# Retention heads' small steps over 14 slots, q's decay in the norm's epsilon, block sums moved into the convolution, two plain groups first

## The chip, the cores and the metric

The program runs on one core of one Trainium2 chip. The time is that of the core in microseconds (us), from the device's own record. The kernel before takes 3146.97 us, the median of three runs. The engines are TensorE (PE in the profile: matmuls; PEld: its weight loads), VectorE (DVE), ScalarE (ACT), GpSimd (POOL) and SyncE (SP), which issues most DMAs from one queue, in order.

## The reference

A decoder trunk of two layers over 2048 positions of width 1024, in float32. Each layer is h + norm(mixer(norm(h))).

The first layer's mixer multiplies the normed input by one weight matrix and splits the columns into 8 retention heads (q and k of 64 columns, v and a gate of 128) and 1024 short-convolution channels (cb, cc, cx and a gate). A head rotates q and k by position, works in chunks of 128 positions and carries a state of 64 x 128:

```
scores = einsum('bnihd,bnjhd->bnhij', qc, kc) * intra      # decay inside a chunk
inner  = einsum('bnhij,bnjhe->bnihe', scores, vc)
cross  = einsum('bnihd,nbhde,hi->bnihe', qc, prev, xi)     # xi[i] = gamma^(i+1)
r = rms_norm(inner + cross, gn)                            # per position and head, eps 1e-6
```

r times silu(gate), beside cb * conv3(cc * cx) * silu(gate), goes through an output matrix. The second layer is latent attention with 8 heads; the change does not touch it.

## The kernel before, in words

**Products.** The input projection is made in groups, Q = 0 to 63. Groups 0 to 31 are the heads: four pairs of heads (768 columns: two times 384) by eight blocks of 256 rows. Groups 32 to 63 are the convolution: 2 x 8 x 2 groups with 512 columns a half. A group multiplies a 2 x 2 block matrix by a 2 x 2 block matrix and needs seven block products instead of eight (`PROD`: P1, P4, P5, P3, P6, P2, P7), because sums of blocks are multiplied: S1 to S4 of the left side, T1 to T4 of the right. P4 and P3 of a group are made during the next group. Each float32 operand is split into a high and a low part (`split`: ScalarE copies the high part, VectorE subtracts), and a product is 4 x 3 = 12 matmuls (`mm12`, lines 87 to 89).

**Slots.** The order is written out by hand. A slot is one product plus all that is listed for its number: `T0(Q)` is the number of group Q's first slot, seven slots to a group. `step` issues the product and then `slot`: first the small matmuls listed in `pe_ev`, then `prep` (the low part of the left operand for 4 slots ahead, line 308; the high part for 5 ahead, line 300; its load 8 ahead, lines 283 to 290), then the list `events`, then `retention_engine`, then the second halves (`en`) of the small steps. Every engine runs its own part of this in order and waits where it needs another's result. The left operands pass through a ring of nine tiles (`us`). For groups 0 to 7 they are taken from SBUF (`RA`, `SS`), later from DRAM (`a_d`, `s_d`), and for the convolution from `wc_d` (a copy of the weights) and `ws_d` (their sums).

**Weights and sums.** `change` loads and splits the right operands of the next head pair or convolution half around its first group. `job` makes block sums on GpSimd: a load into a tile (w9 or j8 in turn), four additions of 512 columns (lines 373 and 374), a store. Kind "r" makes the T of head pairs, "u" the T of the convolution's right side (the normed input, read from `ub_d`), "w" the S of the convolution's weights. From group 8 a job starts every 4 slots. `cps` copies weights from DRAM to DRAM, one every 4 slots from slot 8.

**The heads' small steps.** Each group gives two units (one per head). Of a unit, `post` rotates q and k on VectorE (lines 512 to 518) and prepares v and the gate (519 to 522); `tr` transposes q and k (527, 528) and moves them out of PSUM: q times its decay xi on VectorE (542), k on ScalarE (543); `score` (551 to 564) makes scores and the chunk's addition to the state; `inner` (572, 573, 585 to 587) makes the outputs and the norm's sum of squares, with `eps` as a constant; `mixed` (593) scales; the transposes at 533 turn the result around, and `mix_tr` copies it out (600) and stores it from GpSimd's queue (601). In slots counted from the next group's first: post in 2 and 4, transposes in 4 and 7, scores in 5 and 8, inner in 7 and 11. So scores follow the transposes by one slot. `g1` puts transposes of one unit, output transposes and inner of others into one break of the products.

**The start.** Group 0 is made of eight plain products (`rows0`) while the input x is normed (`x_rstd`, `x_norm`), transposed (468) and copied out (672), 256 rows to a group; the T of the first head pair are made on GpSimd (760), stored to `wt_d` and loaded back. Groups 1 to 7 get their x tiles the same way some 14 slots ahead; `a_store` writes them to `a_d` and once more, by blocks, to `ub_d` (476).

## Time and profile before

| | |
|---|---|
| median of three runs | 3146.97 us |
| profiled execution | 3142.59 us |
| its span, first to last instruction | 3140.8 us |
| mean granted TensorE clock | 0.984 |
| heads, until the third product of group 32 | 797 us |
| convolution's last product | about 1414 us |

The profile shows one execution. A row of groups reads: line, engine, operation, output<-inputs, shape, xcount | busy us, mean ns of one | idle time before them and what ended it. A row of waits reads: who waited <- for whom: us in total, times, longest. A timeline row begins with its start and duration. A stretch's row gives, per engine, busy us and the number of instructions, then the granted clock (1.00 is full speed), the busy share of the 16 DMA engines and GB/s. SPq and ACTq are the issuing of DMAs on those engines.

### The profile page before, as it was taken

The page shows a single profiled execution, that of the slowest core. Times are in us where ns is not written, and L with a number is a line of the kernel's source. Part 1 is how long each engine was busy: PE and PEld are TensorE (multiplying, and loading weights), DVE is VectorE, ACT ScalarE, POOL GpSimd, SP SyncE. Part 2 cuts the span into 40 slices and gives each one's busy share as a digit, 9 for nine tenths or more (in the row PEclk, how much of TensorE's full clock was granted, in tenths as well). Part 3 has the DMA queues.
Part 4 walks back from the last instruction along what each step waited for, and adds up shares of the span by engine and source line. Part 5 has one row for each costly group of instructions (what it writes and reads, how often), then busy time and mean ns, then how long its engine had stood idle before and what let it go on. Part 6 is the DMA issues. An engine that isn't in the chain of part 4 may idle for free.

```text
span 3140.8 us, 46345 instructions
## 1 busy us (share of the span) xinstructions
PE 2999.4 (95%) x16413; PEld 2628.3 (84%) x16413; DVE 1862.5 (59%) x3687; ACT 1337.0 (43%) x3218; POOL 877.9 (28%) x1271
## 2 busy tenths in 40 slices
PE   4898988889999999998999999999999999999999
PEld 4787877789788888887888888998899999999887
DVE  5777888887655565545333311558666666666643
ACT  4544444445533353334222321343555555555521
POOL 4465666662100000000111110014333333333311
PEclk8999999999999999999999999999999999999999
DMA  6688898974433453336333542426321211212552
GB/s 240 231 274 277 291 326 298 343 258 148 154 110 111 144 171 111 109 94 212 127 121 108 162 145 72 123 82 212 114 66 60 66 52 63 63 51 68 169 162 87
DMA packets 279879, 477.05 MB, mean 152 GB/s; under 512 B 27840, under 2 KB 163664, under 8 KB 274896
## 3 DMA queue, kind: packets, MB, share of 16 engines
q1 hardware_dynamic: 254128, 390.43, 38.7%
q0 software_dynamic: 25200, 83.38, 7.3%
q8 instruction: 130, 2.13, 0.3%
q14 instruction: 101, 0.83, 0.1%
q10 hardware_dynamic: 320, 0.29, 0.0%
HBM read 327.20 MB, written 170.66 MB: 159 GB/s over the span
## 4 chain that ended last, share of the span: by engine, by line
PE 77%; DVE 7%; issue 7%; DMA 5%; POOL 3%; ACT 1%; SPq 1%; POOLq 0%; DVEq 0%; ACTq 0%
PE y L966 11%; PE bx L87 5%; PE fy L1738 5%; PE bx L89 5%; PE bx L88 5%; PE T L1543 4%; PE by L87 2%; PE by L88 2%; PE by L89 2%; PE o L1573 2%; PE o L1572 2%; PE o L1571 2%; PE S L1490 2%; PE S L1493 2%; PE S L1494 2%
## 5 line engine op out<-in xcount | busy, mean ns | idle before, releaser
L1511 POOL TENSOR_SCALAR P<-P,al 128x512 f32<-128x512 f32 (+2 forms) x320 | 218.7, 693 | 353.8 <-DVE al L1516 168.3
L308 DVE TENSOR_TENSOR us<-us 128x512 fp32r<-128x512 f32 x392 | 300.9, 777 | 8.0 <-ACT us L300 4.8
L1501 ACT ACTIVATE P<-S,nm 128x512 f32<-128x512 f32 (+2 forms) x320 | 200.8, 627 | 197.1 <-DVE nm L1498 173.4
L300 ACT CAST us<-us 128x512 fp32r<-128x512 f32 x392 | 233.2, 624 | 70.2 <-DMA us<-s_d 52.1
L1498 DVE TENSOR_REDUCE nm<-S 128x1 f32<-128x512 f32 (+2 forms) x320 | 194.3, 608 | 71.2 <-PE S L1494 43.3
L368 ACT COPY u<-bx 128x512 f32<-128x512 f32 (+1 forms) x126 | 67.1, 533 | 307.1 <-PE bx L89 306.9
L1547 DVE TENSOR_TENSOR TL<-T,TH 128x512 fp32r<-128x512 f32 x224 | 154.3, 689 | 63.4 <-ACT TH L1546 62.2
L1571 PE MATMUL o<-TH,vH 128*128 128x256 f32 x576 | 185.1, 321 | 0.0
L966 PE MATMUL y<-woH,mH 128*128 128x512 f32 x512 | 159.9, 394 | 8.9 <-ACT woH L82 8.9
L1543 PE MATMUL T<-ident,P 128*128 128x128 f32 x1088 | 166.2, 273 | 0.0
L1573 PE MATMUL o<-TH,vL 128*128 128x256 f32 x576 | 162.9, 283 | 0.0
L1572 PE MATMUL o<-TL,vH 128*128 128x256 f32 x576 | 162.1, 282 | 0.0
L966 PE MATMUL y<-woH,mL 128*128 128x512 f32 x512 | 158.5, 391 | 0.0
L966 PE MATMUL y<-woL,mH 128*128 128x512 f32 x512 | 157.6, 389 | 0.0
L83 DVE TENSOR_TENSOR mL<-mr,mH 128x512 fp32r<-128x512 f32 (+1 forms) x72 | 45.3, 631 | 170.0 <-ACT mH L82 170.0
L1546 ACT CAST TH<-T 128x512 fp32r<-128x512 f32 x224 | 131.0, 585 | 24.2 <-PE T L1543 18.6
L899 POOL DMA_DIRECT2D mix_d<-j x32 | 17.3, 540 | 441.2 <-DVE j L898 441.2
L1543 PEld LDWEIGHTS T<-ident,P 128*128 128x128 f32 x1088 | 125.1, 140 | 7.8
L966 PEld LDWEIGHTS y<-woH,mH 128*128 128x128 f32 x512 | 95.4, 189 | 28.2 <-ACT woH L82 9.3
L1490 PE MATMUL S<-kH,aqn 128*128 128x512 f32 (+2 forms) x320 | 118.4, 370 | 0.1
L82 ACT CAST mH<-mr 128x512 fp32r<-128x512 f32 (+1 forms) x72 | 40.9, 569 | 176.3 <-issue 93.6
L1493 PE MATMUL S<-K,aqr 128*128 128x512 f32 (+2 forms) x320 | 115.4, 361 | 0.0
(566 smaller groups left out, 9357.2 us busy)
## 6 DMA issues: line engine op xcount, KB each, us to landing
us<-ws_d SPq DMA_DIRECT2D x128, 256.0 KB, 2.9
us<-s_d SPq DMA_DIRECT2D x96, 256.0 KB, 6.0
us<-wc_d SPq DMA_DIRECT2D x96, 256.0 KB, 2.6
us<-a_d SPq DMA_DIRECT2D x72, 256.0 KB, 6.0
wc_d<-in_even_w_conv SPq DMA_DIRECT2D x32, 512.0 KB, 5.8
qn_d<-qn POOLq DMA_DIRECT2D x32, 512.0 KB, 3.2
aqn<-qn_d SPq DMA_DIRECT2D x64, 256.0 KB, 3.1
mr<-mix_d SPq DMA_DIRECT2D x56, 256.0 KB, 2.7
```

The source lines that it names most:

```text
L87: PE.matmul(o, ah, bh, start=first, stop=False, **kw)
L88: PE.matmul(o, ah, bl, start=False, stop=False, **kw)
L89: PE.matmul(o, al, bh, start=False, stop=last, **kw)
L300: A.copy(ring[n_][:, 0], f32(ring[n_][:, 1]))
L308: V.tensor_tensor(out=t_[:, 1], in0=src, in1=f32(t_[:, 0]), op=ALU.subtract)
L966: PE.matmul(ys[t][i], a, w[k][:, i * 512:(i + 1) * 512], start=first and pi == 0, stop=last and pi == 2)
L1501: later(D_EXP, lambda: A.activation(p_[:, 0:w], sp[:, 0:w], AF.Exp, bias=nm[:, j:j + 1], accum_out=sm[:, j:j + 1]))
L1511: G.tensor_scalar(t_[:, 0:ww], t_[:, 0:ww], al[:, jj:jj + 1] if n > 1 else al[:, 5:6], al[:, 5:6] if n > 1 else 1.0, op0=ALU.mult, op1=ALU ...
L1543: PE.transpose(tp[:, e, z, :], src, ident)
L1571: PE.matmul(hold[i], vH[h][:, kb, :], pth[:, c], start=first, stop=False)
L1572: PE.matmul(hold[i], vH[h][:, kb, :], ptl[:, c], start=False, stop=False)
L1573: PE.matmul(hold[i], vL[h][:, kb, :], pth[:, c], start=False, stop=last)
```

## The change

- The first two groups, not one, are plain products; the seven-product scheme begins with group 2. The sums S of groups 0 and 1 are made in place on GpSimd after their products' operands have been split (`s_op0`), and the T of the first head pair on VectorE (`t_op`). The norm's weights are loaded first, from ScalarE's queue, and the second x tile before the projection weights.
- The decay xi of q is no longer multiplied in. A row of the output is then larger by 1/xi, and the norm divides that out if its epsilon is scaled by 1/xi^2: a table `c_epsx` replaces the constant. q leaves PSUM by two ScalarE copies.
- A unit's steps are listed over 14 slots: transposes in 3 and 6, scores in 5 and 8, inner in 7 and 10, output transposes of two units together in 9, `mixed` in 8 and 13. Outputs are stored from ScalarE's queue, and the tile vh has two buffers instead of three. The transposes of x (468) use the PSUM bank that product P2 writes (`a`) instead of that of the q and k transposes.
- Jobs start every 7 slots instead of every 4; fourteen of them (ten "w", four "u") start after the heads, every 5 slots, in tiles of their own.
- `ub_d` is gone: what was read from it is read from `a_d` in pieces of 512 bytes. The copies of weights are made shortly before use, and half of the second row's copies is left out.

```diff
-    c["c_xi"] = ((g[:, None] ** (i + 1.0)) * DK ** -0.5).astype(np.float32)
+    c["c_epsx"] = (EPS * DK / g[:, None] ** (2.0 * (i + 1.0))).T.astype(np.float32).copy()
...
-        for Q in range(1, NQ_ + 1):
+        for Q in range(2, NQ_ + 1):
...
-        T0 = lambda Q: 7 * (Q - 1)
+        T0 = lambda Q: 7 * (Q - 2)
...
-                    SP.dma_start(flat(L), ub_d[tb, j, :, k0 * 512:(k0 + nk) * 512])
+                    for uu in range(2):
+                        for c in range(2):
+                            o = (2 * uu + c) * P
+                            SP.dma_start(L[:, :, o:o + P], a_d[2 * tb + uu, :, 2 * c + j, k0 * P:(k0 + nk) * P].rearrange("p (k c) -> p k c", k=nk))
...
             def a_store(Q):
                 SP.dma_start(a_d[Q].rearrange("p z c -> p (z c)"), RA[Q].rearrange("p z k c -> p (z k c)"))
-                for z in range(4):
-                    c, j = divmod(z, 2)
-                    o = (2 * (Q % 2) + c) * P
-                    SP.dma_start(ub_d[Q // 2, j].rearrange("p (k t) -> p k t", k=4)[:, :, o:o + P], RA[Q][:, z])
...
-                vh = bp.tile([P, 2, P], F32, tag="vh", bufs=3, name=f"vh_{s}")
+                vh = bp.tile([P, 2, P], F32, tag="vh", bufs=2, name=f"vh_{s}")
...
-                    V.tensor_tensor(out=qT[r, c, :], in0=pt[r, 0, :], in1=xi_[h % 2][r, :], op=ALU.mult)
+                    A.copy(qT[r, c, :], pt[r, 0, :])
                 A.copy(kT, pt[:, 1, :])
...
-                G.tensor_scalar(ss, ss, 1.0 / DV, EPS, op0=ALU.mult, op1=ALU.add)
+                G.tensor_scalar(ss, ss, 1.0 / DV, epsx[:, h:h + 1], op0=ALU.mult, op1=ALU.add)
...
+            def mix_tr(v, pt):
+                lo = 0 if v[0] is not None else 2
+                hi = 4 if v[1] is not None else 2
+                mxo = bp.tile([P, 4, P], F32, tag="mxo", bufs=1, name=f"mxo{v[0]}_{v[1]}")
+                A.copy(mxo[:, lo:hi], pt[:, lo:hi, :])
+                for i, s in enumerate(v):
+                    if s is not None:
+                        h, u = units[s]
+                        A.dma_start(mix_d[h * P:(h + 1) * P, u * 256:(u + 1) * 256], mxo[:, 2 * i:2 * i + 2].rearrange("p c t -> p (c t)"))
...
+            for p in range(RQ):
+                a_, b_ = 2 * p, 2 * p + 1
+                b = T0(p + 1)
+                if p >= 2:
+                    late(T0(p) + 5, lambda p=p: sum_a(p))
+                    late(b, lambda p=p: sum_y(p, 1, 1, "u3"))
+                    late(b + 1, lambda p=p: A.copy(pjt[0][:, 1, :], banks(p, "x")))
+                    late(b + 3, lambda p=p: sum_y(p, 1, 0, "u2"))
+                at(b + 2, lambda a_=a_: post(a_))
+                at(b + 4, lambda b_=b_: post(b_))
+                small(b + 3, *step_tr(a_))
+                small(b + 5, *step_score(a_))
+                small(b + 6, *step_tr(b_))
+                small(b + 7, *step_inner(a_))
+                late(b + 8, lambda a_=a_: mixed(a_))
+                small(b + 8, *step_score(b_))
+                small(b + 10, *step_inner(b_))
+                late(b + 13, lambda b_=b_: mixed(b_))
+                small(b + 9, *step_mix((a_, b_ - 2 if p else None)))
...
-            js += [("w", q_, 0) for q_ in range(8)] + [("u", 1, k) for k in range(4)] + [("w", q_, 0) for q_ in range(8, 16)]
+            js += [("w", q_, 0) for q_ in range(6)]
             for i, (kd, a_, b_) in enumerate(js):
-                job_at(T0(8) + 3 + 4 * i, job(kd, a_, b_, (w9, j8)[i % 2]))
+                job_at(T0(8) + 3 + 7 * i, job(kd, a_, b_, (w9, j8)[i % 2]))
...
-            cps = [(wh_d[h, j], w_heads[h, j]) for hp in range(1, 4) for h, j in ((2 * hp, 0), (2 * hp, 1), (2 * hp + 1, 1))]
-            cps += [(wc_d[o * 8 + ct], w_conv[o * 8 + ct]) for ct in range(8) for o in (2, 1, 3, 0)]
-            for i, (o, a_) in enumerate(cps):
-                at(8 + 4 * i, lambda o=o, a_=a_: SP.dma_start(o, a_))
+            for hp in range(1, 4):
+                for i, (h, j) in enumerate(((2 * hp, 0), (2 * hp, 1), (2 * hp + 1, 1))):
+                    at(T0(8 * hp) - 40 + 6 * i, lambda h=h, j=j: SP.dma_start(wh_d[h, j], w_heads[h, j]))
+            for q_ in range(16):
+                g_, ct, w = CQ[q_]
+                o0, o1 = (o * 8 + ct for o in COFF[w])
+                at(T0(RQ + q_) - 25, lambda o0=o0: SP.dma_start(wc_d[o0], w_conv[o0]))
+                at(T0(RQ + q_) - 22, lambda o1=o1: SP.dma_start(wc_d[o1, 1], w_conv[o1, 1]))
...
             x_load(0)
+            A.dma_start(gpre, pbc(pre_norm[0], D))
             SP.dma_start(ident, c_ident)
-            SP.dma_start(gpre, pbc(pre_norm[0], D))
+            x_load(1)
...
+            def t_op(n_):
+                o, a_, b_ = {"T1": ("B11", "B12", "B11"), "T3": ("B12", "B22", "B12"), "T2": ("B22", "B22", "B11"), "T4": ("B21", "B21", "B22")}[n_]
                 for half in range(2):
+                    c = slice(768 * half, 768 * half + 768)
+                    V.tensor_tensor(out=raw0[o][:, c], in0=raw0[a_][:, c], in1=raw0[b_][:, c], op=ALU.subtract)
+                SP.dma_start(wt_d[0, :, TIX[n_]].rearrange("p k c -> p (k c)"), raw0[o])
...
+            for Q in range(2):
+                C0 = {(c, h): psb.tile([P, 512], F32, tag="xy"[c], bufs=2, name=f"b0{Q}{c}{h}")[:, 0:384] for h in range(2) for c in range(2)}
+                for i, (c, j, h) in enumerate(rows0):
...
+                    mm12(C0[c, h], q0[Q, c, j], lambda k: (H[:, k, :], L[:, k, :]), j == 0, j == 1, False)
+                    early(Q, i)
+                    slot(8 * Q + i - 16)
...
+            jc = [cp.tile([P, 3072], F32, tag="u8", bufs=1, name="jc0"), cp.tile([P, 2048], F32, name="jc1")]
+            for i, (kd, a_, b_) in enumerate([("w", q_, 0) for q_ in range(6, 16)] + [("u", 1, k) for k in range(4)]):
+                job_at(LAST_SMALL + 1 + 5 * i, job(kd, a_, b_, jc[i % 2]))
```

More of the change, by code (lines that the diff above doesn't have):

```diff
@@ L110, in body @@
     wc_d = dram.tile([32, 2, P, 512], F32, name="wc_d")
-    ub_d = dram.tile([4, 2, P, 2048], F32, name="ub_d")
     ws_d = dram.tile([16, P, 4, 512], F32, name="ws_d")
@@ L392, in load @@
                     for z in range(4):
-                        SP.dma_start(t_[:, z], ub_d[2 * a + z % 2, z // 2, :, b * 512:(b + 1) * 512])
+                        j, tb = z // 2, 2 * a + z % 2
+                        for uu in range(2):
+                            src = a_d[2 * tb + uu].rearrange("p (c j) (k t) -> p c j k t", j=2, t=P)[:, :, j, b, :]
+                            SP.dma_start(t_[:, z, uu * 256:(uu + 1) * 256].rearrange("p (c t) -> p c t", c=2), src)
             def store():
@@ L418, in body @@
             qk_ = [bp.tile([P, 2, 2, 64], F32, name=f"qk{i}") for i in range(2)]
-            xi_ = [bp.tile([P, P], F32, name=f"xi{i}") for i in range(2)]
+            epsx = bp.tile([P, HR], F32, name="epsx")
             pjt = [bp.tile([P, 2, 384], F32, name=f"pj{i}") for i in range(2)]
@@ L442, in s_place @@
                 sj["t"] = w_new(7, F32, "sj")
-                SS.update({Q: QB(sj["t"]) for Q in range(1, 7)})
+                SS.update({Q: QB(sj["t"]) for Q in range(2, 7)})
             at(-5, s_place)
@@ L528, in tr_pe @@
                 PE.transpose(pt[:, 1, :], qk[:, 1].rearrange("p c d -> p (c d)"), ident)
-            def mix_pe(s, pt):
-                mc = st.pop(s)["mc"]
-                for c in range(2):
-                    PE.transpose(pt[:, 2 + c, :], mc[:, c, :], ident)
             def tr(s, pt):
@@ new lines, in step_mix, with pe @@
+            def step_mix(v):
+                def pe():
+                    pt = psb.tile([P, 4, P], F32, tag="tr", bufs=1, name=f"tm{v[0]}_{v[1]}")
+                    for i, s in enumerate(v):
+                        if s is not None:
+                            mc = st.pop(s)["mc"]
+                            for c in range(2):
+                                PE.transpose(pt[:, 2 * i + c, :], mc[:, c, :], ident)
+                    return pt
+                return pe, lambda pt: mix_tr(v, pt)
@@ L633, in unit, with step_score, step_inner @@
+            def step_score(s):
+                return lambda: score_pe(s), lambda _: score(s)
+            def step_inner(s):
+                return lambda: inner_pe(s), lambda _: inner(s)
             def unit(s):
                 return s if 0 <= s < NU else None
-            for Q in range(RQ):
-                a_, b_ = 2 * Q, 2 * Q + 1
-                base_t = T0(Q + 1)
-                tail_ = Q == RQ - 1
-                small(base_t + 4, g1(a_, unit(a_ - 1), unit(a_ - 2)))
-                if a_:
-                    at(base_t + 5, lambda a_=a_: mixed(a_ - 1))
-                at(base_t + (7 if tail_ else 8), lambda a_=a_: mixed(a_))
-                small(base_t + 5, (lambda a_=a_: score_pe(a_), lambda _, a_=a_: score(a_)))
-                small(base_t + (6 if tail_ else 7), g1(b_, a_, unit(b_ - 2)))
-                small(base_t + (7 if tail_ else 8), (lambda b_=b_: score_pe(b_), lambda _, b_=b_: score(b_)))
@@ L671, in x_evac @@
+            end = T0(RQ) + 14
+            small(end + 1, *step_mix((None, NU - 1)))
+            LAST_SMALL = end + 1
             def x_evac(Q, c, j, pt):
@@ L697, in body @@
                 at(b - 1, lambda Q=Q: s_store(Q))
+            for Q, b in ((0, -13), (1, -7)):
+                at(b - 1, lambda Q=Q: a_store(Q))
+                for i in range(4):
+                    at(b + i, lambda Q=Q, i=i: s_op0(Q, i, G))
+                at(b + 3, lambda Q=Q: s_store(Q))
             L_ = dict(B11=-14, T1=-13, T2=-6, B21=-4, T3=-2, T4=-1, B22=0)
@@ L796, in body @@
-            C0 = {(0, 0): banks(0, "x"), (1, 0): banks(0, "y")}
-            C0[0, 1] = psb.tile([P, 512], F32, tag="x", bufs=2, name="bx0b")[:, 0:384]
-            C0[1, 1] = psb.tile([P, 512], F32, tag="y", bufs=2, name="by0b")[:, 0:384]
-            rows0 = [(c, j, h) for j in range(2) for h in range(2) for c in range(2)]
             def prep(t_):
```

230 lines of the change are left out of this document (95 added, 135 removed).

## The prediction

> **What bounds the kernel now.** I began with the page's busy times and slices, then cut the span into stretches, each starting at the third product of a group, so that whole groups can be counted.
>
> ```profile
> PE 2999.4 (95%) x16413; PEld 2628.3 (84%) x16413; DVE 1862.5 (59%) x3687; ACT 1337.0 (43%) x3218; POOL 877.9 (28%) x1271
> core 0: us, PE busy (x) PEld busy (x) DVE busy (x) ACT busy (x) POOL busy (x), PEclk, DMA share, GB/s
> 0.00:22.00 22.00, 3.83 (x17) 3.35 (x18) 6.95 (x9) 7.84 (x13) 5.86 (x14) 1.00 0.71 269
> 22.00:65.00 43.00, 23.84 (x122) 22.55 (x121) 32.14 (x24) 18.98 (x33) 27.06 (x21) 0.82 0.58 192
> 65.00:108.50 43.50, 27.89 (x129) 24.23 (x128) 26.88 (x41) 22.67 (x45) 13.34 (x19) 0.75 0.75 270
> 108.50:227.00 118.50, 109.25 (x671) 101.88 (x669) 92.13 (x176) 63.12 (x168) 68.08 (x81) 0.96 0.74 250
> 227.00:257.80 30.80, 21.94 (x124) 19.58 (x120) 18.04 (x39) 11.98 (x31) 12.66 (x16) 0.94 0.94 319
> 257.80:436.50 178.70, 163.30 (x962) 149.22 (x960) 147.10 (x283) 85.87 (x234) 107.42 (x123) 0.97 0.87 297
> 436.50:626.30 189.80, 165.49 (x962) 150.62 (x960) 157.48 (x281) 83.06 (x230) 124.25 (x124) 0.96 0.91 315
> 626.30:699.10 72.80, 63.75 (x364) 59.04 (x360) 58.98 (x104) 32.90 (x90) 51.64 (x51) 0.93 0.80 271
> 699.10:776.10 77.00, 77.00 (x482) 72.73 (x480) 55.98 (x139) 38.95 (x113) 19.47 (x34) 1.00 0.48 144
> 843.30:1414.50 571.20, 570.52 (x2517) 471.95 (x2516) 306.31 (x469) 211.26 (x373) 22.88 (x52) 1.00 0.40 121
> ```
>
> From 843 us on TensorE never rests: a convolution group takes 571.2/30 = 19.04 us, and the change adds or removes no product there. What can be won lies before. The same view for line 89 alone (four matmuls to a product, 28 to a group) counts the groups: 5 from 108.5, 1 from 227.0, 8, 8, 3, and 4 from 699.1.
>
> ```profile
> 108.50:227.00 118.50, 48.38 (x140) 27.41 (x140) 0.96 0.74 250
> 257.80:436.50 178.70, 76.88 (x224) 43.44 (x224) 0.97 0.87 297
> 699.10:776.10 77.00, 37.50 (x112) 21.02 (x112) 1.00 0.48 144
> ```
>
> So the last groups of the heads run at 77.0/4 = 19.25 us with TensorE full and GpSimd idle of jobs. With jobs a group takes 178.7/8 = 22.3 and 189.8/8 = 23.7. Measured against 19.25, the excess is 118.5 - 96.3 = 22.2, 30.8 - 19.3 = 11.5, 178.7 - 154 = 24.7, 189.8 - 154 = 35.8 and 72.8 - 57.8 = 15.0, together 109; some 12 of it are x's transposes in the first six groups (12 tiles, about 1 us each: 24.2/16 = 1.5 by the row of line 468 below, whose ends overlap the next product), so 97 are stalls. Whom TensorE waits for, and who else waits, from 88 to 800 us (total, times, longest):
>
> ```profile
> PE sk L551 <- ACT kT L543: 44.1, 26, 9.3
> PE tr L527 <- DVE qk L518: 23.7, 15, 4.5
> PE bx L88 <- DVE c1B L330: 4.0, 1, 4.0
> ACT kT L543 <- DVE qz L542: 106.0, 57, 4.6
> ACT us L300 <- DMA us<-s_d: 52.1, 19, 6.6
> ```
>
> Scores wait for ScalarE's kT, and kT for VectorE's qT, one product after the transposes. Changing of weights (c1B and its like) takes 8 more, and the rest of the 97, some 21, is matmuls at the lower clock that the column shows wherever there are stalls.
>
> **The steps over 14 slots: the heads.** TensorE's own price, from the timeline at 709 us:
>
> ```profile
> 708.89 0.59 PE L551 MATMUL sk<-qz,kT 128*128 128x256 f32 x2
> 709.78 0.44 PE L87 MATMUL bx<-c3T,us 128*128 128x384 f32 x1
> 711.97 0.33 PE L87 MATMUL bx<-c3B,us 128*128 128x384 f32 x1
> 714.06 0.27 PE L527 MATMUL tr<-ident,qk 128*128 128x128 f32 x1
> ```
>
> A product takes 714.06 - 711.97 = 2.09 us and 2.19 behind a small group: 0.10 for each break. The change keeps every small matmul and makes six breaks of four: 0.2 us a group, 6 us over 30 groups.
>
> Scores come two products after the transposes instead of one: 4.2 us of cover, where kT and the two halves of qT ask ScalarE for three copies at 0.27 (line 543, 17.0 us in 64). I let the 44 us go. The rotated q (line 518) now has two products, a score group, the outputs' transposes and an inner group (6.6 us) ahead of its transposes, where it had three products and a score group (7.3): this wait is not relieved by the order. It is relieved by what slows VectorE:
>
> ```profile
> L374 POOL TENSOR_TENSOR w9x<-w9x 128x512 f32<-128x512 f32 (+1 forms) x56 | 76.7, 1370 | 6.8 <-DVE stt L580 5.0
> 436.50:626.30 189.80, 19.77 (x32) 0.96 0.91 315
> 699.10:776.10 77.00, 5.53 (x16) 1.00 0.48 144
> ```
>
> The last two rows are line 512 alone: 0.62 us each beside jobs, 0.35 without. A job is four GpSimd operations of 1.37, 5.5 us, every 4 slots before and every 7 after, so 5.5 us a group instead of 9.6; VectorE per group goes from 14.0 (55.98/4) without jobs to 19.7 (157.48/8) with them, 1.7 of it weight splits, so 4.0 us for 9.6 of jobs. With 5.5 it loses 2.3, and 35.4 us in all of qT's products leave it:
>
> ```profile
> L542 DVE TENSOR_TENSOR qz<-tr,xi 64x128 f32<-64x128 f32 x124 | 35.4, 285 | 12.2 <-PE tr L533 11.1
> L601 POOL DMA_DIRECT2D mix_d<-mxo x64 | 39.5, 617 | 155.9 <-ACT mxo L600 155.8
> L468 PE MATMUL xp<-ident,xt 128*128 128x128 f32 x128 | 24.2, 324 | 38.3 <-DVE xt L462 16.6 <-ACT j L672 15.7 <-ACT w9x L672 6.0
> 0.87 0.39 ACTq L736 DMA_DIRECT2D rt_b<-in_positions  x1
> ```
>
> That makes 14.0 - 1.1 + 2.3 = 15.2 of 19.5 us. The Trainium skill (GPSIMD Engine Reference, Key points) says that GpSimd shares its SBUF interfaces with VectorE and contends with instructions that have two SBUF inputs. If that were full exclusion, the 4.1 us of jobs taken from a group would give VectorE 4.1 back, not the 1.7 that the rows give; the trace agrees with the direction. I leave half of the qk waits, 12, the 8 of the weight changes, and 6 for the clock. New: outputs of the second unit are scaled one slot before the same PSUM bank is written again, and x's transposes share bank a with one product, so each needs a prompt ScalarE or VectorE. No row shows this; the nearest are the kT waits, 44.1/26 = 1.7 us a time. Bounds 0 and 1.7 in each of 30 groups, 0 to 51; I take 0.5, 15 us, since one product (2.09) covers each. Heads: 97 - (12 + 8 + 6 + 15) - 6 = 50 us won, bounds 5 and 91.
>
> ScalarE takes qT's copies (1.1 us a group) and two issues of 0.39 that cost GpSimd 0.62; with 38.95/4 = 9.7 us busy it has the room. The epsilon from a table is the same GpSimd instruction: nothing. With two vh buffers instead of three, ScalarE waits for the inner group one slot earlier; a product covers that, and behind it on ScalarE stand casts due five slots later: nothing, or that product's 2.1 us a group if ScalarE runs late.
>
> **The start.** Now the first product begins at 22.02, the first of the seven-product scheme at 65.02, and 108.5 us is the third product of group 2. Rows that make it late:
>
> ```profile
> 8.57 1.28 DVE L462 SCALAR_TENSOR_TENSOR xt<-xt,ss,w9x 128x1024 f32<-128x1024 f32 x1 [3.53 <-DMA w9x<-in_pre_norm]
> 16.18 1.06 ACT L455 ACTIVATE w9x<-xt 128x1024 f32<-128x1024 f32 x1
> 22.02 0.67 PE L87 MATMUL bx<-c0B,us 128*128 128x384 f32 x1
> 64.25 1.12 PE L468 MATMUL xp<-ident,xt 128*128 128x128 f32 x4 [10.20 <-ACT j L672]
> 65.02 0.67 PE L87 MATMUL bx<-c0B,us 128*128 128x384 f32 x1
> 73.32 0.83 ACT L329 CAST c0T<-c0T 128x768 fp32r<-128x768 f32 x1 [8.23 <-DMA c0T<-wt_d]
> L476 SPq DMA_DIRECT2D ub_d<-j x16: 525/1258/1948, 30.3 to 187.8; - x16
> SPq L387 <- DMA ws_d<-w9x: 28.0, 6, 6.8
> ```
>
> The norm's weights come first and the second x tile is squared ahead of the weight split instead of at 16.18; that brings the first product to about 15. Group 1 as eight plain products needs no difference matrices, so eight more products lie over the write and read of T1 that shows as the 8.23. From 15 on: 16 plain products 33.4, group 2's first 2.1, six x tiles at 1 to 1.5 (8), group 0's small steps 19.25 - 7 x 2.09 = 4.6, the slow clock (0.82 and 0.75 above) 5: 68. Remaining waits: the sums of groups 0 and 1 are made in place, so group 2's tiles can't be written until group 0's store has landed, which is the 10.20 row's kind; I take 4. So 72 instead of 108.5: 36 won. Bounds 62 (no waits, no slow clock) and 95 (both 8 to 10 us waits stay and VectorE, which takes over the T differences, lags as much again): 13 to 46. The 32 issues to ub_d of 1.26 us leave SP's queue.
>
> **The convolution.** Fourteen jobs move here, one per 5 slots (13.6 us): 5.5 us of GpSimd; VectorE is busy 306/571. Traffic: 121 GB/s now, 2.1 MB per job 154, the w_conv copies, 0.79 MB per group, 41: 316 GB/s for 190 us, as much as the heads carried at 315 from 436 to 626 us, where the waits list names no late ring tile for TensorE. Three weights read as 512-byte pieces cost SP eight issues instead of two, at most 10 us by the L476 row, against a lead of 8 slots, 22 us. SP is in order, so ring loads also stand behind a job's load that waits for an earlier store (28.0 us in 6, longest 6.8, in the last row): 10 + 6.8 still fits into 22. Cost 2; bounds 0 and 36, the whole excess of that stretch.
>
> **Sum.** The profiled execution took 3142.59 us (span 3140.8), 4.4 below the median of 3146.97. 50 + 36 - 2 = 84: 3058 by the profile, 3062 as a median.
>
> **Rivals.**
> *The floor is reached* (0.15): no new waits in the heads, 91, and 40 at the start: 131, so 3016. For it: 699 to 776 us shows a full TensorE with the old, tighter order. Against it: 626 to 699, jobs half gone, still loses 15.
> *VectorE stays the pace* (0.17): only kT's 44 minus 15 and 6, and 23 at the start: 46, so 3101. For it: line 512's 0.62; weight splits still fall into two groups at each change. Against it: 15.2 of 19.5.
> *The clock sags* (0.05). If six short breaks a group keep the heads at the 0.93 of the stretch from 626 us, 24 groups x 19.45 x 0.07 = 33 more: 3095. Against it: 1.00 from 699 to 776 with four breaks. The Trainium skill (TensorE: Matmul & The Clock Gate, A second HAM failure mode: psum-queue depth-cycling) describes frequent micro-idles between matmul groups making the clock fall back; the 1.00 speaks against it here.
> *ScalarE becomes the late one* (0.08), slower. It now makes kT, qT, the output copies and their DMA issues in order behind casts that wait for ring tiles (52.1 us in 19 waits, longest 6.6). If each of 60 units meets a 6.6 us wait where 4.2 - 0.8 = 3.4 is covered, 3.2 x 60 = 192 replaces the 97: with 6 for breaks and 36 from the start, 65 slower, 3212. It passes today's time once the loss goes over 127 us, 40 of 60 units. Against it: the copies, jobs and ub_d that make these loads late mostly leave the heads.
>
> **Numbers.** The forecast has 0.55, its own range 3035 to 3085. About 2%, 63 us, is what a measurement of this kernel tells from no change: 3084 and 3210. Faster: 0.50 of the forecast, 0.15 and 0.02 of the rest: 0.67. Slower by over 2%: half of the last rival and some mishap, 0.06. Same: 0.27. The range 3012 to 3118 takes in the floor and VectorE's pace and leaves out the slow rival and the tails.
>
> **What would show it.** Third product of group 2 near 72 us; groups of 20 to 21 us from then on while jobs run and 19.5 without; scores' wait for kT (or qT) under 10 us in all; line 512 near 0.5; convolution groups still 19.04 us. Wrong it would be if groups stay above 22 us, if ScalarE's wait for ring tiles grows, or if convolution groups lengthen while jobs run there.

## The result

The changed kernel takes 3056.61 us (median of 4 runs, 3055.22 to 3058.16) against 3147.03 for the one before: a ratio of 0.9711, 95% interval 0.9694 to 0.9727, so 90 us less. (One of the four runs behind 3147.03 was a slow one of 3374.76 us, and one of the four of the order-back kernel below took 5548.9 us at a granted clock of 0.83; neither enters a ratio.) The profiled execution took 3055.22 us for a span of 3053.4. The forecast was 3062 and 84 us less; the total holds, the main reason it gave for the heads doesn't.

The busy times on the page of the changed kernel:

```profile
PE 2976.4 (97%) x16425; PEld 2615.8 (86%) x16425; DVE 1788.4 (59%) x3557; ACT 1371.5 (45%) x3312; POOL 849.1 (28%) x1203
```

TensorE's busy time fell by 23 us although it makes one product more (group 1 takes eight plain ones instead of seven): much of the time at a lower granted clock is gone from the start and the heads. The span fell by 87.4, so the other 64 were idle time.

The span cut again at third products of groups: group 2 at 75.40, then 7, 8, 10, 14, 17, 22, 26, 30 and, at 753.60, 34. Columns as before: the stretch and its length, busy time of each engine, granted clock, DMA share, GB/s.

```profile
14.00:75.40 61.40, 51.46 (x275) 47.31 (x273) 51.97 (x56) 38.05 (x75) 32.42 (x34) 0.92 0.77 281
75.40:187.90 112.50, 105.47 (x656) 99.12 (x654) 84.38 (x162) 71.26 (x187) 63.28 (x69) 0.97 0.50 175
187.90:223.20 35.30, 21.20 (x123) 18.53 (x121) 20.01 (x38) 16.01 (x40) 14.49 (x19) 0.89 0.84 293
223.20:267.30 44.10, 41.01 (x243) 37.57 (x241) 33.88 (x65) 25.16 (x66) 21.47 (x24) 0.97 0.60 187
267.30:344.40 77.10, 77.10 (x482) 72.85 (x480) 51.99 (x118) 38.95 (x116) 34.21 (x38) 1.00 0.77 229
344.40:413.00 68.60, 62.26 (x363) 57.08 (x361) 54.44 (x101) 42.50 (x111) 35.64 (x34) 0.95 0.82 267
413.00:509.40 96.40, 96.40 (x603) 91.05 (x601) 67.82 (x151) 51.45 (x151) 46.55 (x55) 1.00 0.74 231
509.40:591.90 82.50, 78.20 (x483) 72.72 (x481) 68.62 (x129) 51.15 (x135) 47.67 (x46) 1.00 0.78 265
591.90:669.00 77.10, 77.10 (x482) 72.84 (x480) 50.55 (x120) 40.68 (x121) 18.67 (x26) 1.00 0.56 154
753.60:944.20 190.60, 190.60 (x844) 157.86 (x843) 116.86 (x150) 69.44 (x121) 86.59 (x75) 1.00 0.90 294
```

Read it by group. Five groups from 413.00 take 96.4 us, 19.28 each, with jobs on GpSimd; four from 591.90, 19.28 with hardly any. In both PE is busy for the whole stretch. What is lost is in few places: the groups around changes of weights (8 to 10, 14 to 17, 22 to 26), group 2 to 3, and x's transposes up to group 7. Group 8 alone takes 35.3 us.

The third product of group 2 came at 108.5 us and comes at 75.4, 33 won; that of group 32 at 797.2 and 709.3, so the heads between them took 688.7 and take 633.9, 55 won. The third product of group 34, deep enough in the convolution to find TensorE full, comes 89.7 earlier (753.60 for 843.30) and the whole span ended 87.4 earlier: 2 us come back after the convolution.

Waits of the changed kernel from 55 to 740 us (total, times, longest):

```profile
ACT us L299 <- DMA us<-s_d: 31.8, 18, 3.8
PE sk L545 <- DVE stt L574: 18.3, 6, 8.5
PE xp L474 <- DVE pj L646: 6.3, 4, 3.3
ACT c1T L331 <- DMA c1T<-wt_d: 8.9, 1, 8.9
PE r L566 <- DVE mc L587: 5.7, 4, 2.5
PE tr L526 <- DVE qk L517: 3.1, 2, 2.8
```

The scores' wait for kT is no longer in the list, that for the rotated q is 3.1 us, and ScalarE waits less for ring tiles. A new wait heads TensorE's list: scores for VectorE's update of the state (stt), 18.3 us, 8.5 of them in group 8 and the rest around group 2 and the other changes of weights. Why the old waits went is what the experiments are about.

### The profile page after: what moved, and what is told of

The parts are those of the page before. It is cut to its first block, busy times and chain, and to the rows that moved or that the text cites. A ratio compares the mean times of both kernels' runs of the same rounds, so it can differ in the third digit from the quotient of the medians.

```text
span 3053.4 us, 46275 instructions
## 1 busy us (share of the span) xinstructions
PE 2976.4 (97%) x16425; PEld 2615.8 (86%) x16425; DVE 1788.4 (59%) x3557; ACT 1371.5 (45%) x3312; POOL 849.1 (28%) x1203
## 4 chain that ended last, share of the span: by engine, by line
PE 89%; DMA 4%; POOL 2%; DVE 2%; ACT 1%; issue 1%; SPq 0%; POOLq 0%; DVEq 0%; ACTq 0%
PE y L980 11%; PE bx L87 6%; PE bx L88 5%; PE bx L89 5%; PE fy L1752 5%; PE T L1557 4%; PE by L87 3%; PE by L88 3%; PE by L89 3%; PE o L1587 2%; PE o L1586 2%; PE o L1585 2%; PE S L1504 2%; PE S L1507 2%; PE S L1508 2%; PE S L1505 2%
## 5 line engine op out<-in xcount | busy, mean ns | idle before, releaser
L299 ACT CAST us<-us 128x512 fp32r<-128x512 f32 x392 | 235.5, 620 | 103.1 <-DMA us<-s_d 31.8
L980 PEld LDWEIGHTS y<-woH,mH 128*128 128x128 f32 x512 | 95.4, 189 | 28.6 <-ACT woH L82 9.8
```

The source lines that it names most:

```text
L299: A.copy(ring[n_][:, 0], f32(ring[n_][:, 1]))
L980: PE.matmul(ys[t][i], a, w[k][:, i * 512:(i + 1) * 512], start=first and pi == 0, stop=last and pi == 2)
```

## The experiments

Two theories stood at first. **Order**: the new spacing of the small steps lets the waits go; that is the prediction's. **Jobs**: the new spacing changes little, and the gain comes from 14 of 32 jobs leaving the heads and the rest starting every 7 slots. The experiments undo one part each. Differences are between medians; each interval is about 5 us wide to either side.

### Jobs back, order kept

```diff
-            js += [("w", q_, 0) for q_ in range(6)]
+            js += [("w", q_, 0) for q_ in range(8)] + [("u", 1, k) for k in range(4)] + [("w", q_, 0) for q_ in range(8, 16)]
...
-                job_at(T0(8) + 3 + 7 * i, job(kd, a_, b_, (w9, j8)[i % 2]))
+                job_at(T0(8) + 3 + 4 * i, job(kd, a_, b_, (w9, j8)[i % 2]))
...
-            for i, (kd, a_, b_) in enumerate([("w", q_, 0) for q_ in range(6, 16)] + [("u", 1, k) for k in range(4)]):
-                job_at(LAST_SMALL + 1 + 5 * i, job(kd, a_, b_, jc[i % 2]))
```

> The changed kernel with all 32 jobs back in the heads, one every 4 slots, and none in the convolution. If the order of the small steps is what removed the waits (order theory), scores still have two products to wait in, and the heads lose only the part of the q and k waits that the prediction left to GpSimd: 5 to 15 us, 3062 to 3072. If GpSimd's jobs slowing VectorE were the cause (GpSimd theory), the groups from 8 to 26 go back to 22 us and more: 35 to 50 us, 3092 to 3107. VectorE per group in the stretch of groups 16 to 24 rises from 15.3 to about 17 us in both.

3115.83 us (3106.52 to 3118.13), 0.9904 [0.9888, 0.9920]: 59 slower than the changed kernel. With the new order in place, the jobs alone take back two thirds of the gain. The waits of this kernel from 200 to 700 us:

```profile
ACT us L299 <- DMA us<-s_d: 78.0, 34, 6.6
ACT us L299 <- DMA us<-a_d: 39.3, 16, 5.7
PE r L566 <- DVE mc L587: 26.7, 7, 5.6
PE bx L87 <- ACT u L370: 15.7, 7, 4.1
PE sk L545 <- ACT kT L537: 2.6, 2, 1.4
```

and, in the same view, those of SP's queue:

```profile
SPq L389 <- DMA ws_d<-j: 23.1, 6, 5.3
SPq L389 <- DMA ws_d<-w9x: 22.2, 5, 6.3
```

kT is on time, as the order promises, and TensorE waits elsewhere: for the scaled outputs (line 587) and for ScalarE's evictions. ScalarE itself waits 117 us for ring tiles, and SP's queue waits at line 389, a job's load, for an earlier job's store out of the same tile. One place shows how the two hang together. SP's timeline (start, duration), then ScalarE's and TensorE's, with the idle time before and who ended it in brackets:

```profile
521.99 0.56 SPq L406 DMA_DIRECT2D uc_d<-w9x  x1
529.42 5.13 SPq L398 DMA_DIRECT2D w9x<-a_d  x8
534.65 1.03 SPq L282 DMA_DIRECT2D us<-s_d  x2
```

```profile
540.06 0.62 ACT L299 CAST us<-us 128x512 fp32r<-128x512 f32 x1 [4.87 <-DMA us<-s_d]
541.30 0.46 ACT L370 COPY u<-bx 128x384 f32<-128x384 f32 x1
541.81 0.62 PE L87 MATMUL bx<-c2T,us 128*128 128x384 f32 x1 [3.99 <-ACT u L370]
```

The store of tile w9x is issued at 521.99. The next job's load into w9x waits for that store to land (4.6 us of it at the head of the queue) and goes out at 529.42, in eight pieces that take 5.13 us to issue. The ring tile's load stands behind them in SP's queue, goes out at 534.65, and ScalarE, which works in order, stands 4.87 us before the cast at 540.06. Its copy of a finished product out of PSUM comes behind that cast, and TensorE's next product into the bank stands 3.99 us. Such a wait needn't get through in full: after ScalarE stood 5.22 us before its cast at 524.81, TensorE lost 1.24 us, at 528.01. With a job every 4 slots and two tiles a tile is loaded again two slots after its store, 5.5 us at 19.25/7 = 2.75 us a slot; such a store takes 7.0 us to land in this kernel. At every 7 slots it is loaded again eight slots later, 22 us.

### Jobs alone, on the kernel before

The new start times of the jobs put into the kernel before, which otherwise stays (a weight tile `u8` had to be cut otherwise, to make room for the convolution's job tiles).

```diff
-            js += [("w", q_, 0) for q_ in range(8)] + [("u", 1, k) for k in range(4)] + [("w", q_, 0) for q_ in range(8, 16)]
+            js += [("w", q_, 0) for q_ in range(6)]
...
-                job_at(T0(8) + 3 + 4 * i, job(kd, a_, b_, (w9, j8)[i % 2]))
+                job_at(T0(8) + 3 + 7 * i, job(kd, a_, b_, (w9, j8)[i % 2]))
...
+            for i, (kd, a_, b_) in enumerate([("w", q_, 0) for q_ in range(6, 16)] + [("u", 1, k) for k in range(4)]):
+                job_at(LAST_SMALL + 1 + 5 * i, job(kd, a_, b_, jc[i % 2]))
```

> The kernel before with one part of the change alone: 18 jobs every 7 slots in the heads and 14 during the convolution; old order of the small steps, q's decay on VectorE, old start, weights still copied early and ub_d kept. If the jobs carry the heads' gain (jobs theory, which the run with the jobs put back suggests), nearly all of the heads' 55 us is won: 3090 to 3105. If the order and the fewer jobs are both needed, less than half: above 3120.

3103.53 us (3102.22 to 3106.53), 0.9869 [0.9854, 0.9885]: 42 less than the kernel before, with the old order and the old start. Its third products of groups 8, 16, 24 and 27 bound these stretches; the two lines of the second fence are its waits from 88 to 760 us. The third has TensorE's waits between the third products of groups 8 and 27, two rows for the kernel before and two for this one, and the fourth VectorE's line 512, as in the prediction.

```profile
258.90:426.80 167.90, 158.03 (x963) 147.22 (x961) 134.02 (x283) 84.04 (x232) 81.83 (x98) 0.99 0.81 265
426.80:592.30 165.50, 158.52 (x962) 148.01 (x960) 130.59 (x281) 83.16 (x231) 86.50 (x102) 0.98 0.81 269
592.30:658.00 65.70, 59.26 (x362) 54.31 (x360) 52.25 (x106) 33.42 (x91) 37.39 (x42) 1.00 0.68 218
```

```profile
PE sk L551 <- ACT kT L543: 41.2, 20, 8.4
ACT us L300 <- DMA us<-s_d: 15.2, 11, 5.9
```

```profile
PE tr L527 <- DVE qk L518: 23.1, 14, 4.5
PE sk L551 <- ACT kT L543: 20.6, 17, 3.4
PE sk L551 <- ACT kT L543: 14.8, 11, 2.4
PE tr L527 <- DVE qk L518: 5.0, 4, 1.3
```

```profile
426.80:592.30 165.50, 11.56 (x32) 0.98 0.81 269
```

The same groups took 178.7, 189.8 and 72.8 us: 42 us won, all of it between groups 8 and 27, where the jobs run. ScalarE's wait for s_d's ring tiles falls from 52.1 to 15.2 us. Of the wait for kT 41.2 us are left, hardly less than the 44.1 of before, but 26 of them lie ahead of the third product of group 8, where none of the moved jobs has begun. In the stretch of the jobs the wait for the rotated q falls most, from 23.1 to 5.0, that for kT from 20.6 to 14.8, and TensorE's busy time for the same products from 392.5 to 375.8 at a higher granted clock: together 41 of the 42 us. Line 512 takes 0.36 us instead of the 0.62 of before. So in the old kernel the jobs cost by way of VectorE, slower beside them, which makes the rotated q and also qT, behind which ScalarE copies kT. The path through late ring tiles, seen above, matters little here: between groups 8 and 27 of the old kernel VectorE stood 4.6 us for ScalarE's casts of ring tiles, against 65.6 with the jobs put back into the new one.

### Order back

```diff
-                small(b + 3, *step_tr(a_))
+                small(b + 4, *step_tr(a_))
...
-                small(b + 6, *step_tr(b_))
+                small(b + 7, *step_tr(b_))
```

> The changed kernel with the q and k transposes one slot later (4 and 7), so that scores follow by one product as before; nothing else differs. Order theory: the 44 us of the scores' wait come back, or somewhat less since qT and kT are now made on one engine: 20 to 44 us, 3077 to 3100. GpSimd theory: with fewer jobs VectorE and ScalarE answer in time, 0 to 10 us, 3057 to 3067.

3056.07 us, 0.9719 [0.9703, 0.9735]: no difference. Its wait from 55 to 740 us:

```profile
PE sk L545 <- ACT kT L537: 4.3, 3, 3.5
```

The scores stand one product behind the transposes again, as before, and wait 4.3 us in all. The prediction's order theory falls: with the rest of the change in place, one product is cover enough, in the groups ahead of the jobs too.

### q's decay on VectorE again

`qT` is multiplied by a loaded xi on VectorE, as before, and the norm has its constant epsilon.

```diff
-                    A.copy(qT[r, c, :], pt[r, 0, :])
+                    V.tensor_tensor(out=qT[r, c, :], in0=pt[r, 0, :], in1=xi_[h % 2][r, :], op=ALU.mult)
...
-                G.tensor_scalar(ss, ss, 1.0 / DV, epsx[:, h:h + 1], op0=ALU.mult, op1=ALU.add)
+                G.tensor_scalar(ss, ss, 1.0 / DV, EPS, op0=ALU.mult, op1=ALU.add)
```

> The changed kernel with q's decay multiplied in again on VectorE and a constant epsilon. Order theory: two products cover two 0.29 us multiplications, 0 to 5 us, 3057 to 3062. If taking 35 us from VectorE and the hop between the engines was the cause, ScalarE waits for VectorE again at each unit and the scores wait with it: 20 to 40 us, 3077 to 3097.

3064.42 us (3060.49 to 3066.12), 0.9742 [0.9726, 0.9758]: 8 slower, between the two expectations. The two copies on ScalarE are worth 8 us, most of which shows as a longer stall at the first weight change (from group 7's product P2 to group 9's it takes 62.5 us instead of 56.5) rather than as a wait for qT.

```profile
PE sk L548 <- ACT c1T L331: 11.3, 1, 11.3
```

### All three back

Jobs, decay and order undone together.

> The three together: all jobs every 4 slots in the heads, q's decay on VectorE, scores one product after the transposes. If these three carry the heads' gain, it goes: 50 to 55 us, 3107 to 3112. If the three only cover the same slack, the sum of the three single losses is much smaller than this one. If the rest of the change (late copies of weights, no ub_d, output transposes of two units together, the late scaling) carries it, below 25 us, under 3082.

3131.07 us (3127.31 to 3133.93), 0.9957 [0.9942, 0.9972]: 74 slower; the three alone make 59 + 8 + 0 = 67. Here, from 200 to 700 us, the kT wait is back, and ScalarE's for s_d's ring tiles is shorter (51.8) than with the jobs alone put back (78.0):

```profile
PE sk L548 <- ACT kT L540: 62.5, 20, 10.5
```

So order and decay together do let this wait go where jobs crowd, but in the kernel with all jobs other waits of nearly the same size take its place. With the three parts undone the third product of group 32 comes at 781.5 us, 16 before the old kernel's, though group 2's came 32 earlier: whatever else was changed in the heads (outputs' transposes, stores from ScalarE) costs some 17 us under the old load of jobs. Which of it does wasn't tried.

### What in a job costs: transfers, GpSimd, or the queue

Four kernels take the 59 us of the first experiment apart. First, all jobs at every 4 slots, but without the sums on GpSimd (except those of the second head pair); the loads and stores stay.

```diff
-            return [load] + job_ops(t_, kind) + [store]
+            return [load] + (job_ops(t_, kind) if (kind, a) == ("r", 1) else [lambda: None] * 4) + [store]
```

> All 32 jobs every 4 slots in the heads, as in the run with the jobs put back, but without GpSimd's additions (except those of the second head pair, whose jobs run before group 8): the loads and stores alone, so the sums are left out and T and S are raw weights. If the moving of data is what costs (traffic theory: ring tiles land late, and ScalarE waits for them in order), most of the 59 us stays: 40 to 59, 3097 to 3116. If GpSimd's additions slowing VectorE cost it (GpSimd theory), it falls to the changed kernel's time or below: 3045 to 3060.

3089.58 us (3085.92 to 3091.74), 0.9822 [0.9806, 0.9838]: 33 of the 59 stay with the transfers alone. ScalarE's waits for ring tiles from 200 to 700 us are longer here than with the sums:

```profile
ACT us L299 <- DMA us<-s_d: 91.8, 40, 5.3
ACT us L299 <- DMA us<-a_d: 61.5, 23, 7.0
```

That is 153 us against 117, in a kernel that is 26 us faster. So the length of this wait is no price by itself: it costs what TensorE loses behind it. Second, the changed kernel with three more additions on GpSimd beside each job of the heads (a tile of their own, no transfer), so that GpSimd has as many as with a job every 4 slots:

```diff
+                for o_ in (0, 1, 2):
+                    at(T0(8) + 3 + 7 * i + o_, lambda: G.tensor_tensor(out=dj, in0=dj, in1=dj, op=ALU.add))
```

> The changed kernel with three more GpSimd additions of 128 x 512 in each job's 7 slots, on a tile of their own, so that GpSimd adds once in every slot from group 8 to 26 as it did before; no transfer is added. GpSimd theory: line 511 goes back to 0.6 us and the time to 3095 to 3116. Traffic theory: VectorE is busier, TensorE hardly waits: 0 to 10 us, 3057 to 3067.

3072.50 us (3071.29 to 3073.83), 0.9769 [0.9755, 0.9784]: 16 slower, between the two expectations. Line 511 of the changed kernel (one of VectorE's multiplications for the rotated q and k, 513 here) shows what GpSimd's work does to VectorE. The changed kernel, then transfers alone, then more GpSimd, then the first experiment, with all jobs and their sums; total and count behind the length:

```profile
392.00:550.60 158.60, 16.53 (x32) 1.00 0.77 254
```

```profile
400.00:590.00 190.00, 10.54 (x34) 0.96 0.89 293
```

```profile
395.00:560.00 165.00, 22.11 (x32) 0.98 0.73 240
```

```profile
407.30:605.50 198.20, 16.01 (x32) 0.94 0.84 278
```

That is 0.52, 0.31, 0.69 and 0.50 us each. The Trainium skill (GPSIMD Engine Reference, Key points) says that GpSimd shares its SBUF interfaces with VectorE and contends with instructions that have two SBUF inputs, as line 511 has; the first three rows agree. The last one shows that the number of additions doesn't set the size: the first experiment adds as often as the third row's kernel, and its line 511 is no slower than the changed kernel's. So these 16 us are not GpSimd's share of the 59. And a slower VectorE costs nothing in a quiet group. The kernel with more GpSimd, five groups away from a change (421.3 on), then the first of the two groups in which it loses (the other is 560.5 to 589.1), and in the second fence, from the timeline, the wait in it:

```profile
421.30:517.80 96.50, 96.50 (x603) 91.14 (x601) 71.86 (x149) 51.28 (x151) 61.89 (x66) 1.00 0.74 232
391.80:421.30 29.50, 22.75 (x122) 20.93 (x120) 24.94 (x35) 15.20 (x37) 20.26 (x18) 0.88 0.56 200
```

```profile
414.54 0.80 PE L568 MATMUL r<-vh,at 128*128 128x128 f32 x2 [5.02 <-DVE mc L589]
```

96.5 for five groups is what the changed kernel takes. The groups of 29.5 and 28.6 us (20.9 each in the changed kernel) hold all of the 16 us: there VectorE and GpSimd also split weights. In the first of them VectorE works from 398 to 415 us without a pause, some of its operations drawn out (line 307 takes 0.7 to 2.3 us), and so scales the outputs late; its wait for the norm's factors is 2.1 us there.

Third, all jobs at every 4 slots again, sums and all, but their transfers are issued from GpSimd's queue and not SP's; the same bytes at the same slots.

```diff
-                        SP.dma_start(t_[:, z], w_conv[COFF[w][r] * 8 + ct, kh])
+                        (SP if (kind, a) == ("r", 1) else G).dma_start(t_[:, z], w_conv[COFF[w][r] * 8 + ct, kh])
```

(and so at the five other places of `job`)

> All 32 jobs every 4 slots in the heads as in the run with the jobs put back (3116), but their loads and stores are issued from GpSimd's queue instead of SP's, so that the loads of ring tiles no longer stand behind a job's load that waits for an earlier store. The bytes are the same. If SP's order made the ring tiles late (queue theory), ScalarE's wait for them falls from 117 us between 200 and 700 us to below 60 and the time by 15 to 35, to 3080 to 3100. If the traffic itself delays the landings (bandwidth theory), the wait stays above 90 and the time at 3105 to 3130, GpSimd's issuing (0.6 us each, 5 to 9 per job) being added.

3157.74 us (3155.64 to 3159.06), 1.0035 [1.0024, 1.0047]: the slowest of all, and yet it answers the question. Waits from 200 to 700 us:

```profile
ACT us L299 <- DMA us<-s_d: 2.3, 1, 2.3
DVE mc L587 <- POOL rss L581: 108.0, 22, 14.1
```

and one row of its groups of instructions there (busy, mean ns of one, idle before):

```profile
L398 POOL DMA_DIRECT2D j<-a_d x32 | 23.2, 728 | 3.1 <-DMA wt_d<-j 1.5 <-DMA uc_d<-j 1.2 <-DMA ws_d<-j 0.4
```

ScalarE's 117 us of waiting for ring tiles are down to 2.3. The loads land 4.4 us (median) after their issue, for 5.7 in the first experiment, against a lead of eight slots, 22 us. So those loads weren't late for want of bandwidth, but for their place in SP's queue, behind a job's load that waits and takes its time to issue. The waiting has moved to GpSimd, which now stands before the jobs' loads and spends 0.73 us on issuing each piece of a "u" job's load (last row; SP takes 0.61), and the norm's factors that it makes come 108 us late for VectorE. The Trainium skill (DMA: Bandwidth & Descriptors, Issuing engines are not separate DMA queues) says that issuing from several engines saves only the sequencer's time for issuing. By that rule alone the ring loads would have gained the 5.13 us of issuing in the place shown above; the measurement shows more, since the 4.6 us of waiting before the issue were taken from SP's queue too.

Fourth, all jobs every 4 slots from SP, with each store one slot earlier:

```diff
-        def job_at(t_, j_, gap=3):
+        def job_at(t_, j_, gap=2):
```

> All 32 jobs every 4 slots in the heads (3116), but a job's sums and its store are listed one slot earlier after its load, so that the next load into the same tile comes three slots (about 8 us) behind the store instead of two (about 5.5); bytes, GpSimd's additions and the rate of jobs are the same. Stores land in 5 to 7 us. Queue theory: SP's waits for a job's own stores (some 125 us between 200 and 700 us with the jobs put back, 118 before, 5 in the changed kernel) fall below half, ScalarE's waits for ring tiles with them (117 to about 70), and the time by 10 to 25, to 3091 to 3106. Bandwidth theory: both stay, 3110 to 3120. If GpSimd now waits for loads and its norm factors come late, the gain is eaten: DVE mc waits for POOL rss show it.

3101.91 us (3099.96 to 3108.37), 0.9858 [0.9841, 0.9874]: 14 less than with the store at its old slot. A tile is now loaded again three slots after its store, 8.2 us instead of 5.5 against a landing of 7.0. Waits from 200 to 700 us:

```profile
ACT us L299 <- DMA us<-s_d: 55.9, 17, 5.3
ACT us L299 <- DMA us<-a_d: 21.4, 11, 6.5
SPq L389 <- DMA ws_d<-j: 7.5, 6, 2.7
```

SP's wait at line 389 for j falls from 23.1 to 7.5 us, and ScalarE's from 117 to 77. One slot of distance is worth about a quarter of what the jobs cost here. The 77 us that stay suggest that the store's landing is only a part of what holds the ring loads.

### Smaller parts

x's transposes in the bank of the q and k transposes instead of `a`:

```diff
-                xs = [(Q, c, j, x_tr(2 * Q + c, j, "a")) for Q, c, j in xev.get(t_, [])]
+                xs = [(Q, c, j, x_tr(2 * Q + c, j, "tr")) for Q, c, j in xev.get(t_, [])]
```

> The changed kernel with x's transposes in the PSUM bank of the q and k transposes, as before, instead of bank a. In groups 3 to 7 TensorE waits some 1.2 us a group at x's first transpose behind VectorE's sum over bank a (6.3 us in 4 waits). If that wait is the bank's, it goes: 5 us, 3050 to 3053; if ScalarE's copies of q and k then hold the bank, nothing or up to 5 us more: 3056 to 3062.

3063.47 us (3062.01 to 3064.45), 0.9730: 7 slower. Groups 3 to 6 take 23.1 us instead of 22.2. Bank `a` costs the 6.3 us of the xp row above and saves more.

The first loads in their old order (norm's weights behind the identity on SP, the second x tile behind the projection weights):

```diff
-            A.dma_start(gpre, pbc(pre_norm[0], D))
             SP.dma_start(ident, c_ident)
-            x_load(1)
+            SP.dma_start(gpre, pbc(pre_norm[0], D))
```

> The changed kernel with the norm's weights again behind the identity on SP's queue and the second x tile loaded only after the small tables. The prediction gave these two moves some 7 us of the first product's begin (14.0 against 22.0 us now). If the start hangs on the first product, the third product of group 2 comes 3 to 7 us later, 3060 to 3064. If it hangs on VectorE's and ScalarE's work until group 2 (52 of 61 us busy on VectorE) or on T1's way through DRAM, the delay is taken up: 0 to 2 us.

3058.18 us (3056.68 to 3062.93), 0.9728 [0.9709, 0.9747]: no difference. Group 2's third product comes at 77.0 instead of 75.4. The start's gain isn't made by the first loads, so it is left with the second plain group and what goes with it, which wasn't tried by itself.

Group 8 of the changed kernel stands for 8.5 us before its scores: VectorE's update of the state is late behind its split of c1T, and that behind ScalarE's wait for c1T (8.9 us in the waits above). SP's timeline there:

```profile
208.29 0.53 SPq L404 DMA_DIRECT2D wt_d<-xt  x1
212.71 0.32 SPq L316 DMA_DIRECT2D c1T<-wt_d  x1
```

c1T is read from what four jobs write to wt_d; the last store goes out at 208.29 and c1T's load when it has landed. I tried to bring the chain forward: the second job's load ahead of the first one's store, and group 7's sums on VectorE so that GpSimd is free for it.

```diff
+            r1 = [job("r", 1, k, xt_[:, 1536 * ((k + 1) % 2):]) for k in range(4)]
+            at(T0(8) - 12, r1[1][0])
...
-                G.tensor_tensor(out=o, in0=a_, in1=b_, op=op)
+                (V if Q == 7 else G).tensor_tensor(out=o, in0=a_, in1=b_, op=op)
```

> The changed kernel with the block sums for the second head pair begun earlier: the second job's load is listed one slot earlier, ahead of the first job's store, and group 7's S sums go from GpSimd to VectorE, so that GpSimd is free for the jobs. Group 8 now begins 35.2 us after group 7, 16 above the floor, because T1 lands only at about 220 us and ScalarE stands waiting for it with kT behind. If the chain load, sums, store, load sets that, T1 lands 5 to 10 us earlier and the kernel is faster by as much: 3046 to 3052. If another thing is late next (weights B11, the small steps), 0 to 3 us.

3055.68 us (3053.65 to 3057.29), 0.9707 [0.9692, 0.9721]: nothing that can be measured. Its last store goes out at 207.59 and c1T's load at 211.99, 0.7 us sooner. The slots of the last job set the time, not the two things moved; how far they can be pulled forward stays open.

## Why the prediction came out as it did

**The heads: right in size, wrong in the main step.** 50 us were forecast and 55 came. The step that failed is "Scores come two products after the transposes instead of one" with "I let the 44 us go". Undoing that order costs nothing, while undoing the jobs costs 59 and doing the jobs alone wins 42. The waits view named 44 us of waits for kT, but they don't price the order: the old kernel with slower jobs keeps 41 of them and is 42 us shorter, and the new one with the old order has 4.3. The view was also cut wider than the excess that it was to explain: one wait of 9.3 us lies between 88 and 108.5 us, ahead of the 97, so only 34.8 belonged to it.

Between the third products of groups 8 and 27 the change wins 53 us (441.3 to 388.0). The jobs alone make 42 of them there; the other 11 weren't told apart. Ahead of that, groups 3 to 7 went from 118.5 to 112.5 us, and group 8 lost 4.5. Which part of the change took the kT waits there wasn't told apart; the order alone isn't it, nor are the jobs. How the jobs cost depends on the kernel. In the old one they cost through VectorE. In the new one with the jobs put back, part of the cost is the way that the timeline above shows (a ring load behind a job's load in SP's queue, then ScalarE in order, then whoever needs ScalarE), some 30 of TensorE's 64 us of waits between 223 and 660 us by my estimate, which follows each wait back in the trace from releaser to releaser. The prediction had the rows for SP's queue, 28.0 us at line 387, and ScalarE's 52.1 for ring tiles, and used both only to bound the convolution and the slow rival.

**VectorE.** This step held, and was given too little. The prediction said of the rotated q that what slows VectorE relieves it, and let half of its 24 us go; 3.1 are left, and the jobs alone take 18 of 23 on the old kernel. Its working gives 14.0 + 2.3 = 16.3 us a group there, with qT still on VectorE, and 130.59/8 is 16.3. For the changed kernel 15.2 was forecast and line 512 near 0.5; measured 0.52 for that line (511 now), and 67.82/5 = 13.6 us a group in the five quiet groups.

**What was left.** The terms for what stays were spread evenly, 12 for the rotated q, 15 for new hazards, 6 for breaks and 8 for the weight changes. Measured, the quiet groups lose next to nothing: 19.28 with six breaks against 19.25 with four, so two more breaks cost 0.03 us and not 0.2. The rotated q waits 3.1 us; of the hazards x's bank shows 6.3 and the scaled outputs 5.7, while the scores' 18.3 for the state were on no list. The groups at changes of weights were mis-sized the other way: group 8 and the two after it take 79.4 us for 57.8, 344.40 to 413.00 takes 68.6 for 57.8, 509.40 to 591.90 82.5 for 77.0, at 19.25 a group. That is 21.6 + 10.8 + 5.5 = 38, whatever the wait, where 8 was left for the changes. Errors of opposite sign made the sum come out; that is luck. Three figures of the working are slips of no weight: 97 - (12 + 8 + 6 + 51) - 6 is 14 and not 5, the start without waits and slow clock is 63 and not 62, and 3146.97 less 84 is 3063.

**The start.** 36 forecast, 33 measured, third product at 75.4 for 72. The first plain product begins at 14.04 us, for 15 forecast, but the loads' order isn't what wins it. From 14 to 75.4 us the clock is 0.92. Group 3 shares the loss: 26.3 us after group 2, 4 above the groups with transposes that follow.

**The convolution.** Cost 2 forecast. Ten groups with jobs take 190.6 us, 19.06 each for 19.04, PE busy throughout, at a DMA share of 0.90 and 294 GB/s (316 forecast). The lead of eight slots hides them, as argued. The 2 us given back come after the convolution, and weren't followed further.

**The rivals.** ScalarE as the late one (3212) did not come: its waits for ring tiles fell from 52.1 to 31.8 us for `s_d`, as the argument against it said. The kernel with all jobs has the wait that it named, 117 us, and still takes only 3116. The clock doesn't sag with six breaks: 1.00 in every quiet stretch. The floor (3016) is missed by 36 us in the heads, where the groups at changes of weights alone lose 38, and by 7 at the start.

**What stays open.** Transfers alone make 33 of the jobs' 59 us. The other 26 go with GpSimd's sums, and how they do isn't shown: the 16 us of added GpSimd work come with a line 511 of 0.69 us, which the kernel with the jobs put back, at 0.50, hasn't. Nor was it shown what made the heads 17 us slower than before with all three parts undone, or what in the start wins.

## What to carry to other kernels

Price a background job by every queue that it stands in: where its load must wait for an earlier store from the same tile, each transfer behind it on that in-order queue is late by the rest of the store's landing, so let the distance from store to next load exceed the landing time that the profile shows (here 7.0 us against 5.5, then 8.2, then 22). Count what the last engine loses by it and not the lateness itself, which was 153 us in a kernel 26 us faster than one with 117. The wait that TensorE's row names may be only where lateness from elsewhere arrives: follow it back past the named engine before crediting its removal to a new order. When several edits were made at once, undo one and also do one alone; a right total is no proof of the reasons.

## What the runs showed of the hardware

- The same bytes issued from another queue left ScalarE 2.3 us of waiting for ring tiles instead of 117: at 0.81 DMA share over that half millisecond (SP's version; 0.74 in the other) the place in the queue, behind loads that wait (4.6 us in the place shown) and take time to issue (5.13), made them late, and not the transfer rate.
- A DMA share of 0.90 for 190 us beside a TensorE that never rests cost nothing measurable.
- Two more changes between large and small matmuls per group cost 0.03 us a group.
- VectorE's multiplication of line 511 took 0.31, 0.52 and 0.69 us with the jobs' additions on GpSimd left out, four of them in 7 slots, and four plus three on a tile of their own; but 0.50 with the seven of jobs at every 4 slots. Quiet groups took 19.3 us with four and with seven.
- In the stretches shown here the granted clock is below 1.00 only where TensorE stalls: with the jobs alone slowed on the old kernel, its busy time for the same products fell from 392.5 to 375.8 us.
